# Newton's temporaries of the norms in PSUM, and two kinds of elementwise work moved from GpSimd to the vector engine

## The chip, the cores and the metric

One core of a Trainium2 chip. The metric is the device time of one execution of the program in microseconds (us); lower is better. The engines are named as the profile names them: PE is TensorE (matmuls), PEld its weight loads, DVE the vector engine, ACT the scalar engine, POOL GpSimd, SP the engine that issues most DMAs.

## What is computed

512 tokens of 1024 features go through two post-norm layers (feed forward, a mixer, feed forward, a gated addition) and then a block of attention and experts. The norms are what the change touches:

```python
def layer_norm(x, g, b):
    mu = jnp.mean(xf, axis=-1, keepdims=True)
    var = jnp.mean(jnp.square(xf - mu), axis=-1, keepdims=True)
    return (xf - mu) * lax.rsqrt(var + LN_EPS) * g + b

for i in range(DEPTH):                                   # DEPTH = 2
    h = layer_norm(DN_ALPHA * h + 0.5 * swiglu(h, ...), ln_g[i, 0], ln_b[i, 0])
    ...
    h = layer_norm(DN_ALPHA * h + mix, ln_g[i, 1], ln_b[i, 1])
    h = layer_norm(DN_ALPHA * h + 0.5 * swiglu(h, ...), ln_g[i, 2], ln_b[i, 2])
    h = h + (p[i] @ ple_w_proj[i]) * jax.nn.sigmoid(h @ ple_w_gate[i])
```

The second block begins with an RMS norm (`x * rsqrt(mean(x*x) + eps) * g`), has one before its experts, and ends with one.

## The kernel before

**Layout.** Features lie on partitions and tokens along the row, so an activation is eight tiles of 128 x 512. Every product runs in three matmuls (L258, L259, L260): both sides are split into a high part, which is a cast on ACT, and a low part, the rest after it. For weights that is `w()`: a DMA, the cast (L235, ACT) into `wh`, and the subtraction (L236) into `wl`, on DVE unless the caller names GpSimd. `wh` and `wl` are rings of six tiles each, so a cast also waits until the weight six tiles earlier is used up.

**A tail.** A norm needs sums over the features, that is, over partitions. `stat_add` keeps two running sums over the eight tiles, of the values (L308) and of their squares (square on ACT, L299; addition on DVE, L309). `tail` does the last four feature tiles in two halves of 256 tokens. When the first half of all four is done, and the first tile of the second, `sums` adds the running sums over the partitions by matmuls against ones (L316 for values, L317 for squares), which gives 128 x 2 values in a PSUM bank, and `rstd` turns these into one over the deviation and the scaled mean: a chain of 17 instructions of 128 x 2 elements on DVE, each using the result of one before it (L348 to L354 for the variance, L324 to L335 for three Newton steps by `rsqrt`, L357 for the mean). `diagonals` (L383) writes the results onto diagonals, `spread` (L374) multiplies those by ones, so that every partition has the values of all tokens, and the norm is two DVE operations (L425, L426), two on ACT (L429, L430) and a subtraction on POOL (L434) for each tile. Meanwhile PE works on the second half. Its chain is cut into steps that are put between the norm operations of the first half, and its spread comes inside the first products of the next phase (`dense_halves`), whose first half of tokens needs only the first half of the norm.

**Which tails there are.** Six layer norms: at 376 us (feed forward, then the first mixer), 597 (mixer, then feed forward), 974 (feed forward, then the gated addition), and the same three in the second layer at 1410, 1650 and 2026. A seventh tail, at 2099, is the RMS norm after the last gated addition; its chain has 13 instructions and no sum of values. The router's norm and the last norm use the same code without halves.

**Who does what.** In the halves of a tail, the addition to the sum of values (L308) runs on POOL, and so do the low parts (L236) of the third and fourth of the four weights that `opening` fetches for a phase's first products; those of the first two run on DVE. There are seven openings with four weights each.

**Order.** The code is traced as written, and a scheduler then sets the order on each engine by its own estimate of durations; each engine runs its list strictly in that order.

Of the kernel before, what the change touches and what calls it, by code (L numbers as in the profile page):

```python
# [139 lines left out]
class K:  # L140
# [17 lines left out]
    def begin(self):  # L158
        """The input, its splits, and the first weights, by what the first products need."""
# [58 lines left out]
    def old(self, j):  # L218
        """Room of long use: tables of the states, then distances and masks, then the routing."""
# [19 lines left out]
    def narrow(self, src, n):  # L239
        """A function that gives the weights of n columns by their number, out of wide loads of several."""  # L240
# [27 lines left out]
    def mark(self):  # L268
        """The instruction traced last."""
# [3 lines left out]
    def after(self, ins):  # L273
        """What is traced here is issued after ins (an order of issue, not a wait)."""
# [14 lines left out]
    def stat_add(self, st, y, c=FULL, mean=True):  # L289
        """Adds the columns c of y, and of its square, to the sums over the feature tiles."""  # L290
# [12 lines left out]
        if mean:  # L303
# [3 lines left out]
            else:  # L307
                (nc.vector if c == FULL else nc.gpsimd).tensor_tensor(st["s1"][:, c], st["s1"][:, c], y[:, c], ALU.add)  # L308
# [11 lines left out]
    def rsqrt(self, v, n):  # L320
        """1 / sqrt(v) by Newton's steps from a guess by the exponent; a generator, a step at a time."""
        nc = self.nc
        i, y, h, q = self.sm(n, I32), self.sm(n, I32), self.sm(n), self.sm(n)
        nc.vector.tensor_scalar(i, v.bitcast(I32), 1, None, op0=ALU.arith_shift_right)  # L324
        yield
        nc.vector.tensor_scalar(y, i, -1.0, 1597463007.0, op0=ALU.mult, op1=ALU.add)  # L326
        yield
        nc.vector.tensor_scalar(h, v, -0.5, None, op0=ALU.mult)  # L328
        y = y.bitcast(F32)
        for _ in range(3):  # L330
            nc.vector.tensor_tensor(q, y, y, ALU.mult)  # L331
            yield
            nc.vector.tensor_tensor(q, q, h, ALU.mult)  # L333
            yield
            nc.vector.scalar_tensor_tensor(y, q, 1.5, y, op0=ALU.add, op1=ALU.mult)  # L335
            yield
        return y

    def rstd(self, ps, n, eps, mean):
        """1 / deviation, and the mean in its units, negated; a generator."""  # L340
        nc = self.nc
        v = self.sm(n)
        if not mean:
            nc.vector.tensor_scalar(v, ps[:, 4:4 + n], 1.0 / D, eps, op0=ALU.mult, op1=ALU.add)
            yield
            return [(yield from self.rsqrt(v, n))]
        mu, m2, m = self.sm(n), self.sm(n), self.sm(n)
        nc.vector.tensor_scalar(mu, ps[:, :n], 1.0 / D, None, op0=ALU.mult)  # L348
        yield
        nc.vector.tensor_tensor(m2, mu, mu, ALU.mult)  # L350
        yield
        nc.vector.scalar_tensor_tensor(v, ps[:, 4:4 + n], 1.0 / D, m2, op0=ALU.mult, op1=ALU.subtract)
        yield
        nc.vector.tensor_scalar(v, v, 0.0, eps, op0=ALU.max, op1=ALU.add)  # L354
        yield
        r = yield from self.rsqrt(v, n)
        nc.vector.scalar_tensor_tensor(m, mu, -1.0, r, op0=ALU.mult, op1=ALU.mult)  # L357
        return [r, m]
# [8 lines left out]
    def spread(self, cs, dg=None):  # L367
        """Columns [P, 2] of per-token values, each as rows of 256 tokens on every partition, side by side."""
# [17 lines left out]
    def tail(self, st, work, norm, mean=True, end=lambda: None):  # L386
        """The last four feature tiles of a sum and the norm over all, in halves of the tokens: while work(i, half) of the second half runs,
        the first half is normalised. The norm of the second half waits in self.pending."""
# [28 lines left out]
    def layer_norm(self, y, H, g, b):  # L417
        """The norm, in place, and its splits to H, for tail()."""
# [27 lines left out]
    def dense_halves(self, ws, H, then=None):  # L446
        """dense() for up to four weights over H, whose second half of the tokens may be pending. then: called for each half."""
# [15 lines left out]
    def opening(self, srcs):  # L463
        """The weights of a phase's first products."""
        return [self.w(src, 1024, self.nc.gpsimd if n > 1 else None) for n, src in enumerate(srcs)]

# [8 lines left out]
    def ffn(self, X, H, i, ln, then=None, ws=None):  # L475
        """then: called some way before the end. ws: the first weights."""
# [78 lines left out]
    def ple(self, X, H, i, norm=None):  # L555
        """norm: column of the gains of an RMS norm that follows."""
# [96 lines left out]
    def s5_prep(self):  # L653
# [32 lines left out]
        # f = (a - 1) / lambda  # L686
# [18 lines left out]
        # powers a^2 .. a^8  # L705
# [26 lines left out]
        # phase and decay tables over the 64 chunks  # L732
# [18 lines left out]
        # stacked power tables  # L751
# [86 lines left out]
    def s5(self, uT, q):  # L838
        """z for the 128 channels of quarter q, features on partitions; a generator, a stage at a time."""
# [1240 lines left out]
```

## Time and profile before

| | |
|---|---|
| time of three runs | 2836.44, 2845.91 (median), 2849.08 us |
| span of the profiled execution | 2846.9 us |
| mean granted TensorE clock | 0.970 of full |
| PE busy | 2696.5 us, 95% |
| DVE busy | 1494.1 us, 52% |
| ACT busy | 987.0 us, 35% |
| POOL busy | 431.8 us, 15% |

The profile is of one execution; its span is within 0.1% of the median, so what follows is added up against 2846.9 us. The engines work side by side: PE is the one that is nearly always busy, and the others matter where PE waits for them. A wait shows as idle time in front of an instruction, with the instruction that ended it. Durations of DVE instructions in the timeline include time in which the instruction had started and could not go on.

### The profile page before, as it was taken

How to read it: one execution, taken by the hardware profiler on the slowest of the kernel's cores; microseconds unless marked ns; L12 is line 12 of the kernel's file. 1: busy time of each engine (PE TensorE's matmuls, PEld its weight loads, DVE VectorE, ACT ScalarE, POOL GpSimd, SP SyncE). 2: the span in 40 equal slices, each digit the busy share in tenths (PEclk: the TensorE clock that was granted, in tenths of full speed). 3: DMA queues.
4: the chain of work that ended last, by engine and by line, in shares of the span. 5: the costliest groups of instructions: out<-in, count | busy, mean ns of one | idle time of the engine just before them, and what ended most of it. 6: DMA issues, size and time to landing. Idle time of an engine off the chain costs nothing. (4 is left out here: it accounts for less than half of the span.)

```text
span 2846.9 us, 37003 instructions
## 1 busy us (share of the span) xinstructions
PE 2696.5 (95%) x14221; PEld 2170.3 (76%) x14221; DVE 1494.1 (52%) x2966; ACT 987.0 (35%) x1717; POOL 431.8 (15%) x441
## 2 busy tenths in 40 slices
PE   9999989999999899999987999999889999969996
PEld 8888888888888798888875788888788777754443
DVE  5856364564333555333589663333677666553435
ACT  4332242343222353222252452222445544322111
POOL 2101031030000140000157030000234222010000
PEclk9999998999999999999998999999999999979998
DMA  6434216523233223223231123333233222669994
GB/s 216 151 118 142 89 60 182 160 66 113 97 95 96 91 69 119 95 90 98 81 108 62 60 74 98 92 103 93 72 101 110 92 78 79 221 211 364 398 400 156
DMA packets 123826, 370.14 MB, mean 130 GB/s; under 512 B 14592, under 2 KB 14656, under 8 KB 123648
## 3 DMA queue, kind: packets, MB, share of 16 engines
q1 hardware_dynamic: 112688, 333.10, 35.2%
q0 software_dynamic: 10384, 33.61, 3.2%
q8 instruction: 112, 1.84, 0.3%
q10 hardware_dynamic: 576, 1.05, 0.1%
q14 instruction: 66, 0.54, 0.1%
HBM read 343.32 MB, written 24.39 MB: 129 GB/s over the span
## 5 line engine op out<-in xcount | busy, mean ns | idle before, releaser
L258 PE MATMUL p<-a,wh 128*128 128x512 f32 (+1 forms) x3480 | 1276.6, 367 | 0.0
L259 PE MATMUL p<-a,wh 128*128 128x512 f32 (+1 forms) x3480 | 1264.6, 363 | 0.1
L260 PE MATMUL p<-a,wl 128*128 128x512 f32 (+1 forms) x3480 | 1263.6, 363 | 0.0
L235 ACT CAST wh<-wr 128x1024 fp32r<-128x1024 f32 (+2 forms) x399 | 409.1, 1031 | 1109.9 <-PE p L259 786.0
L258 PEld LDWEIGHTS p<-a,wh 128*128 128x128 f32 x3480 | 665.3, 191 | 111.2 <-issue 8.6
L259 PEld LDWEIGHTS p<-a,wh 128*128 128x128 f32 x3480 | 666.1, 191 | 102.4 <-issue 3.6
L260 PEld LDWEIGHTS p<-a,wl 128*128 128x128 f32 x3480 | 665.2, 191 | 101.2 <-issue 1.2
L236 DVE TENSOR_TENSOR wl<-wr,wh 128x1024 fp32r<-128x1024 f32 (+1 forms) x366 | 444.7, 1218 | 405.3 <-ACT wh L235 359.7
L308 POOL TENSOR_TENSOR a<-a,a 128x256 f32<-128x256 f32 x48 | 35.1, 732 | 1328.5 <-DVE a L504 815.2
L497 DVE TENSOR_TENSOR a<-a,p 128x512 f32<-128x512 f32 x88 | 60.5, 687 | 252.4 <-PE p L260 242.7
L504 DVE SCALAR_TENSOR_TENSOR a<-p,a 128x512 f32<-128x512 f32 (+1 forms) x112 | 68.8, 614 | 200.4 <-PE p L260 200.4
L1178 ACT ACTIVATE a<-a,s 128x256 f32<-128x256 f32 (+3 forms) x128 | 67.2, 526 | 73.3 <-DVE s L1176 73.2
L829 POOL DMA_DIRECT2D spill<-a x76 | 42.5, 561 | 330.3 <-DVE a L1448 98.1
L253 DVE TENSOR_TENSOR a<-a,a 128x512 fp32r<-128x512 f32 x120 | 81.9, 689 | 9.8 <-ACT a L252 9.5
L236 POOL TENSOR_TENSOR wl<-wr,wh 128x1024 fp32r<-128x1024 f32 (+1 forms) x33 | 78.8, 2392 | 44.7 <-ACT wh L235 44.7
L299 ACT ACTIVATE a<-a 128x256 f32<-128x256 f32 (+1 forms) x93 | 45.2, 487 | 98.1 <-DVE a L504 44.2
L252 ACT CAST a<-a 128x512 fp32r<-128x512 f32 x120 | 73.6, 621 | 15.5 <-DVE a L497 6.6
L434 POOL TENSOR_TENSOR a<-a,a 128x256 fp32r<-128x256 f32 x96 | 71.5, 759 | 48.3 <-ACT a L430 47.8
L429 ACT ACTIVATE a<-a,vec 128x256 f32<-128x256 f32 x96 | 56.3, 599 | 64.3 <-DVE a L426 64.3
L1908 PE MATMUL p<-we,a 128*64 128x512 f32 x288 | 63.7, 592 | 0.0
L1947 PE MATMUL p<-a,sel 128*128 128x512 f32 x256 | 62.0, 398 | 0.1
L309 DVE TENSOR_TENSOR a<-a,a 128x256 f32<-128x256 f32 (+1 forms) x87 | 53.5, 615 | 12.5 <-ACT a L299 12.1
(423 smaller groups left out, 2523.8 us busy)
## 6 DMA issues: line engine op xcount, KB each, us to landing
wr<-in_w_dram SPq DMA_DIRECT2D x204, 512.0 KB
we<-in_wgu_dram SPq DMA_DIRECT2D x72, 512.0 KB
wr<-in_w_dram SPq DMA_DIRECT2D x64, 448.0 KB
a<-in_wgu_dram SPq DMA_DIRECT2D x112, 256.0 KB
spill<-a POOLq DMA_DIRECT2D x76, 256.0 KB, 3.4
a<-spill SPq DMA_DIRECT2D x76, 256.0 KB
we<-in_wd_dram SPq DMA_DIRECT2D x36, 512.0 KB
wr<-in_win_dram SPq DMA_DIRECT2D x31, 512.0 KB
```

What stands on the lines that cost most here:

```text
L235: nc.scalar.copy(hi[:, :n], raw[:, :n])
L236: (low or nc.vector).tensor_tensor(lo[:, :n], raw[:, :n], hi[:, :n].bitcast(F32), ALU.subtract)
L252: self.nc.scalar.copy(hi[:, :n], x)
L253: (low or self.nc.vector).tensor_tensor(lo[:, :n], x, hi[:, :n].bitcast(F32), ALU.subtract)
L258: mm(o, l[0], r[0], start=start, stop=False)
L259: mm(o, l[0], r[1], start=False, stop=False)
L260: mm(o, l[1], r[0], start=False, stop=stop)
L434: nc.gpsimd.tensor_tensor(l[:, c], y[d - 2][:, c], h[:, c].bitcast(F32), ALU.subtract)
L504: nc.vector.scalar_tensor_tensor(Y[d][:, c], o[:, c], 0.5, Y[d][:, c], op0=ALU.mult, op1=ALU.add)
L1178: nc.scalar.activation(s[x], s[x], AF.Exp, bias=nm[:, x:x + 1], accum_out=z[:, x:x + 1])
L1908: nc.tensor.matmul(o[CAP * i:CAP * i + CAP], xT[k // 4][:, a:a + CAP], wg[k], start=k == 0, stop=k == DT - 1)
L1947: nc.tensor.matmul(o, sels[b][:n, j * P:(j + 1) * P], y[h][i][:n], start=b + i == 0, stop=i == 1 and b == len(blocks) - 1)
```

## The change

`rstd` and `rsqrt` keep the variance, minus half of it and the product in each Newton step in unused columns of the PSUM bank that holds the sums; the guess, the mean and its square stay in SBUF. The formulas are rescaled so that each instruction has at most one input from PSUM and the count stays the same: 17 with a mean, 13 without. (The last norm calls `rsqrt` without a bank and keeps SBUF temporaries.) `stat_add` puts the addition to the sum of values on DVE in the halves too, and `opening` no longer names GpSimd for the low parts.

```diff
@@ stat_add
-                (nc.vector if c == FULL else nc.gpsimd).tensor_tensor(st["s1"][:, c], st["s1"][:, c], y[:, c], ALU.add)
+                nc.vector.tensor_tensor(st["s1"][:, c], st["s1"][:, c], y[:, c], ALU.add)
@@ rstd, rsqrt
-    def rsqrt(self, v, n):
-        i, y, h, q = self.sm(n, I32), self.sm(n, I32), self.sm(n), self.sm(n)
-        nc.vector.tensor_scalar(i, v.bitcast(I32), 1, None, op0=ALU.arith_shift_right)
-        nc.vector.tensor_scalar(y, i, -1.0, 1597463007.0, op0=ALU.mult, op1=ALU.add)
-        nc.vector.tensor_scalar(h, v, -0.5, None, op0=ALU.mult)
-        for _ in range(3):
-            nc.vector.tensor_tensor(q, y, y, ALU.mult)
-            nc.vector.tensor_tensor(q, q, h, ALU.mult)
-            nc.vector.scalar_tensor_tensor(y, q, 1.5, y, op0=ALU.add, op1=ALU.mult)
-    def rstd(self, ps, n, eps, mean):
-        v = self.sm(n)
-        mu, m2, m = self.sm(n), self.sm(n), self.sm(n)
-        nc.vector.tensor_scalar(mu, ps[:, :n], 1.0 / D, None, op0=ALU.mult)
-        nc.vector.tensor_tensor(m2, mu, mu, ALU.mult)
-        nc.vector.scalar_tensor_tensor(v, ps[:, 4:4 + n], 1.0 / D, m2, op0=ALU.mult, op1=ALU.subtract)
-        nc.vector.tensor_scalar(v, v, 0.0, eps, op0=ALU.max, op1=ALU.add)
-        r = yield from self.rsqrt(v, n)
-        nc.vector.scalar_tensor_tensor(m, mu, -1.0, r, op0=ALU.mult, op1=ALU.mult)
+    def rstd(self, ps, n, eps, mean):
+        v, h, q = (ps[:, 16 + 8 * x:16 + 8 * x + n] for x in range(3))
+        s1, s2 = ps[:, :n], ps[:, 4:4 + n]
+            mu, m2 = self.sm(n), self.sm(n)
+            nc.vector.tensor_scalar(mu, s1, -1.0 / D, None, op0=ALU.mult)
+            nc.vector.tensor_tensor(m2, s1, mu, ALU.mult)
+            nc.vector.tensor_tensor(v, s2, m2, ALU.add)
+            nc.vector.tensor_scalar(v, v, 0.0, D * eps, op0=ALU.max, op1=ALU.add)
+            nc.vector.tensor_scalar(v, s2, D * eps, None, op0=ALU.add)
+        r = yield from self.rsqrt(v, n, (h, q))
+        nc.vector.tensor_tensor(m, mu, r, ALU.mult)
+    def rsqrt(self, v, n, room=None):
+        h, q = room or (self.sm(n), self.sm(n))
+        y = self.sm(n)
+        nc.vector.tensor_scalar(q.bitcast(I32), v.bitcast(I32), 1, None, op0=ALU.arith_shift_right)
+        nc.vector.tensor_scalar(y.bitcast(I32), q.bitcast(I32), -1.0, 1597463007.0, op0=ALU.mult, op1=ALU.add)
+        nc.vector.tensor_scalar(h, v, -0.5, None, op0=ALU.mult)
+        for k in (1.0, 1.0, math.sqrt(D)):
+            nc.vector.tensor_tensor(q, h, y, ALU.mult)
+            nc.vector.scalar_tensor_tensor(q, q, k, y, op0=ALU.mult, op1=ALU.mult)
+            nc.vector.scalar_tensor_tensor(y, q, 1.5 * k, y, op0=ALU.add, op1=ALU.mult)
@@ opening
-        return [self.w(src, 1024, self.nc.gpsimd if n > 1 else None) for n, src in enumerate(srcs)]
+        return [self.w(src, 1024) for src in srcs]
@@ the last norm
-        ts(v, v, 1.0 / D, 1e-6, op0=ALU.mult, op1=ALU.add)
+        ts(v, v, D * 1e-6, None, op0=ALU.add)
```

Since the scheduler orders the instructions anew, they move. POOL's list loses 62 rows (48 L308 and 14 L236); DVE's gains them. The lines of the changed kernel are a few numbers off: its chain is L328 to L334 (variance), L350 to L360 (Newton), L342 (mean); L387 is the diagonals, L429 and L430 the norm, L508 the sum with the product (L504 before), L378 the spread.

The vector engine in the first tail, just after the sums of the first half, before the change (`p` are PSUM banks, `s` small tiles, `a` activations, `w` weights; numbers are buffers):

```order
L504 SCALAR_TENSOR_TENSOR a_359<-p_3171,a_359 128x256
L348 TENSOR_SCALAR s_3204<-p_3198 128x2
L350 TENSOR_TENSOR s_3205<-s_3204 128x2
L352 SCALAR_TENSOR_TENSOR s_3203<-p_3198,s_3205 128x2
L354 TENSOR_SCALAR s_3203<-s_3203 128x2
L324 TENSOR_SCALAR s_3211<-s_3203 128x2
L309 TENSOR_TENSOR a_2921<-a_2921,a_3194 128x256
L326 TENSOR_SCALAR s_3212<-s_3211 128x2
L328 TENSOR_SCALAR s_3213<-s_3203 128x2
L331 TENSOR_TENSOR s_3214<-s_3212 128x2
L333 TENSOR_TENSOR s_3214<-s_3214,s_3213 128x2
```

and in the changed kernel, from the same place:

```order
L508 SCALAR_TENSOR_TENSOR a_359<-p_3171,a_359 128x256
L328 TENSOR_SCALAR s_3203<-p_3198 128x2
L308 TENSOR_TENSOR a_2954<-a_2954,a_359 128x256
L330 TENSOR_TENSOR s_3204<-p_3198,s_3203 128x2
L236 TENSOR_TENSOR wl_3392<-wr_3390,wh_3391 128x1024
L309 TENSOR_TENSOR a_2921<-a_2921,a_3194 128x256
L332 TENSOR_TENSOR p_3198<-p_3198,s_3204 128x2
L508 SCALAR_TENSOR_TENSOR a_361<-p_3224,a_361 128x256
L334 TENSOR_SCALAR p_3198<-p_3198 128x2
L308 TENSOR_TENSOR a_2954<-a_2954,a_361 128x256
L350 TENSOR_SCALAR p_3198<-p_3198 128x2
L236 TENSOR_TENSOR wl_3398<-wr_3396,wh_3397 128x1024
```

Behind each of the two L236 there (third and fourth weight of the opening) stand steps of the chain, and the additions of the sum of values (L308) stand between them; the chain's operands are now `p`.

The vector engine at the end of the second half's chain in the same tail, before and after; the two `wl` are the weights that follow the opening's:

```order
L333 TENSOR_TENSOR s_3352<-s_3352,s_3351 128x2
L335 SCALAR_TENSOR_TENSOR s_3350<-s_3352,s_3350 128x2
L357 SCALAR_TENSOR_TENSOR s_3334<-s_3332,s_3350 128x2
L236 TENSOR_TENSOR wl_3559<-wr_3557,wh_3558 128x1024
L383 TENSOR_SCALAR a_3450<-const,s_3350 128x128 x2
L383 TENSOR_SCALAR a_3450<-const,s_3334 128x128 x2
```

```order
L356 TENSOR_TENSOR p_3312<-p_3312,s_3343 128x2
L358 SCALAR_TENSOR_TENSOR p_3312<-p_3312,s_3343 128x2
L236 TENSOR_TENSOR wl_3551<-wr_3549,wh_3550 128x1024
L360 SCALAR_TENSOR_TENSOR s_3343<-p_3312,s_3343 128x2
L236 TENSOR_TENSOR wl_3557<-wr_3555,wh_3556 128x1024
L342 TENSOR_TENSOR s_3375<-s_3327,s_3343 128x2
L387 TENSOR_SCALAR a_3442<-const,s_3343 128x128 x2
```

One L236 stood between the chain and the diagonals, the other behind them; now both stand ahead of the diagonals.

PE among the first products of the next phase, where the second half's spread stands (the `ones` row), before and after; `a_3033` to `a_3036` are the sixth and seventh feature tile's split:

```order
L260 MATMUL p_3410<-a_3033,wl_3388 128x256
L258 MATMUL p_3411<-a_3033,wh_3393 128x256
L259 MATMUL p_3411<-a_3034,wh_3393 128x256
L374 MATMUL p_3455<-a_3450,ones 128x512
L260 MATMUL p_3411<-a_3033,wl_3394 128x256
L258 MATMUL p_3412<-a_3033,wh_3399 128x256
L259 MATMUL p_3412<-a_3034,wh_3399 128x256
```

```order
L260 MATMUL p_3402<-a_3035,wl_3380 128x256
L258 MATMUL p_3403<-a_3035,wh_3385 128x256
L259 MATMUL p_3403<-a_3036,wh_3385 128x256
L260 MATMUL p_3403<-a_3035,wl_3386 128x256
L378 MATMUL p_3447<-a_3442,ones 128x512
L258 MATMUL p_3404<-a_3035,wh_3391 128x256
L259 MATMUL p_3404<-a_3036,wh_3391 128x256
```

The spread stands 13 matmuls later in the products than before; there were 30 matmuls between it and the first that needs the second half of the norm, and there are 18.

## Rows read from the trace of the kernel before

**Rows 1.** The page's part 1: engine, busy us (share of the span) x instructions.
```profile
PE 2696.5 (95%) x14221; PEld 2170.3 (76%) x14221; DVE 1494.1 (52%) x2966; ACT 987.0 (35%) x1717; POOL 431.8 (15%) x441
```
**Rows 2.** PE's waits over the whole span: us in total, times, longest.
```profile
PE p L374 <- DVE a L383: 36.1, 10, 5.2
...
PE p L316 <- POOL a L308: 8.3, 6, 1.4
...
PE p L317 <- DVE a L309: 6.6, 3, 4.2
```
**Rows 3.** Timeline of DVE, first tail: start, duration (us), instruction, [idle before <-releaser].
```profile
376.71 0.16 DVE L348 TENSOR_SCALAR s<-p 128x2 f32<-128x2 f32 x1 [0.36 <-PE p L317]
...
377.21 0.16 DVE L352 SCALAR_TENSOR_TENSOR s<-p,s 128x2 f32<-128x2 f32 x1
377.40 2.14 DVE L354 TENSOR_SCALAR s<-s 128x2 f32<-128x2 f32 x1
...
382.59 2.26 DVE L357 SCALAR_TENSOR_TENSOR s<-s,s 128x2 f32<-128x2 f32 x1
384.77 0.47 DVE L383 TENSOR_SCALAR a<-const,s 128x128 f32<-128x128 f32 x2
...
396.21 0.65 DVE L354 TENSOR_SCALAR s<-s 128x2 f32<-128x2 f32 x1
```
**Rows 4.** Timeline of POOL, same tail.
```profile
377.12 2.41 POOL L236 TENSOR_TENSOR wl<-wr,wh 128x1024 fp32r<-128x1024 f32 x1
...
382.49 2.34 POOL L236 TENSOR_TENSOR wl<-wr,wh 128x1024 fp32r<-128x1024 f32 x1
...
391.82 0.73 POOL L308 TENSOR_TENSOR a<-a,a 128x256 f32<-128x256 f32 x1 [4.65 <-DVE a L504]
```
**Rows 5.** Timelines of ACT and PE, same tail: a cast, and PE's first and second spread.
```profile
379.25 1.05 ACT L235 CAST wh<-wr 128x1024 fp32r<-128x1024 f32 x1 [2.04 <-issue]
...
381.40 0.28 PE L259 MATMUL p<-a,wh 128*128 128x256 f32 x1
381.52 0.28 PE L260 MATMUL p<-a,wl 128*128 128x256 f32 x1
386.03 1.67 PE L374 MATMUL p<-a,ones 128*128 128x512 f32 x2 [4.22 <-DVE a L383]
...
403.68 1.13 PE L374 MATMUL p<-a,ones 128*128 128x512 f32 x2 [1.84 <-DVE a L383]
```
**Rows 6.** DVE groups by line and shape: busy, mean ns | idle before.
```profile
L348 DVE TENSOR_SCALAR s<-p 128x2 f32<-128x2 f32 x12 | 1.9, 160 | 10.5 <-PE p L317 10.5
```
**Rows 7.** Timelines of DVE and PE, tail at 974 us (feed forward, then gated addition).
```profile
974.75 0.16 DVE L352 SCALAR_TENSOR_TENSOR s<-p,s 128x2 f32<-128x2 f32 x1
974.83 1.22 DVE L236 TENSOR_TENSOR wl<-wr,wh 128x1024 fp32r<-128x1024 f32 x1
975.97 0.42 DVE L309 TENSOR_TENSOR a<-a,a 128x256 f32<-128x256 f32 x1
976.31 0.16 DVE L354 TENSOR_SCALAR s<-s 128x2 f32<-128x2 f32 x1
...
992.26 2.63 DVE L309 TENSOR_TENSOR a<-a,a 128x256 f32<-128x256 f32 x1
...
994.95 0.58 PE L317 MATMUL p<-ones,a 128*128 128x1 f32 x2 [1.20 <-DVE a L309]
```
**Rows 8.** Stretches: us, engines' busy us, PEclk (granted clock), DMA share, GB/s.
```profile
386.30:389.60 3.30, 3.30 (x12) 2.46 (x12) 1.83 (x7) 1.02 (x2) 0.72 (x1) 0.53 0.70 238
...
993.90:1000.50 6.60, 5.55 (x16) 4.68 (x17) 5.40 (x18) 3.22 (x9) 4.79 (x7) 0.51 0.23 79
...
614.90:621.50 6.60, 6.57 (x32) 6.44 (x31) 4.77 (x17) 4.14 (x10) 4.35 (x7) 0.52 0.00 0
392.60:396.50 3.90, 3.87 (x30) 3.66 (x31) 2.60 (x9) 2.52 (x7) 3.29 (x5) 1.00 0.01 4
```
**Rows 9.** Timeline of DVE, tail at 2099 us (the RMS norm).
```profile
2108.95 1.22 DVE L236 TENSOR_TENSOR wl<-wr,wh 128x1024 fp32r<-128x1024 f32 x1
```

More of the change, by code (lines that the diff above doesn't have):

```diff
@@ L318, in sums @@
         return ps
-    def rsqrt(self, v, n):
+    def rstd(self, ps, n, eps, mean):
         nc = self.nc
-        i, y, h, q = self.sm(n, I32), self.sm(n, I32), self.sm(n), self.sm(n)
-        nc.vector.tensor_scalar(i, v.bitcast(I32), 1, None, op0=ALU.arith_shift_right)
-        yield
-        nc.vector.tensor_scalar(y, i, -1.0, 1597463007.0, op0=ALU.mult, op1=ALU.add)
+        v, h, q = (ps[:, 16 + 8 * x:16 + 8 * x + n] for x in range(3))
+        s1, s2 = ps[:, :n], ps[:, 4:4 + n]
+        if mean:
+            mu, m2 = self.sm(n), self.sm(n)
+            nc.vector.tensor_scalar(mu, s1, -1.0 / D, None, op0=ALU.mult)
+            yield
+            nc.vector.tensor_tensor(m2, s1, mu, ALU.mult)
+            yield
+            nc.vector.tensor_tensor(v, s2, m2, ALU.add)
+            yield
+            nc.vector.tensor_scalar(v, v, 0.0, D * eps, op0=ALU.max, op1=ALU.add)
+        else:
+            nc.vector.tensor_scalar(v, s2, D * eps, None, op0=ALU.add)
+        yield
+        r = yield from self.rsqrt(v, n, (h, q))
+        if not mean:
+            return [r]
+        m = self.sm(n)
+        nc.vector.tensor_tensor(m, mu, r, ALU.mult)
+        return [r, m]
@@ L327, in rsqrt @@
+    def rsqrt(self, v, n, room=None):
+        nc = self.nc
+        h, q = room or (self.sm(n), self.sm(n))
+        y = self.sm(n)
+        nc.vector.tensor_scalar(q.bitcast(I32), v.bitcast(I32), 1, None, op0=ALU.arith_shift_right)
+        yield
+        nc.vector.tensor_scalar(y.bitcast(I32), q.bitcast(I32), -1.0, 1597463007.0, op0=ALU.mult, op1=ALU.add)
         yield
         nc.vector.tensor_scalar(h, v, -0.5, None, op0=ALU.mult)
-        y = y.bitcast(F32)
-        for _ in range(3):
-            nc.vector.tensor_tensor(q, y, y, ALU.mult)
+        for k in (1.0, 1.0, math.sqrt(D)):
+            nc.vector.tensor_tensor(q, h, y, ALU.mult)
@@ L332, in rsqrt @@
             yield
-            nc.vector.tensor_tensor(q, q, h, ALU.mult)
+            nc.vector.scalar_tensor_tensor(q, q, k, y, op0=ALU.mult, op1=ALU.mult)
             yield
-            nc.vector.scalar_tensor_tensor(y, q, 1.5, y, op0=ALU.add, op1=ALU.mult)
+            nc.vector.scalar_tensor_tensor(y, q, 1.5 * k, y, op0=ALU.add, op1=ALU.mult)
             yield
         return y
-    def rstd(self, ps, n, eps, mean):
-        nc = self.nc
-        v = self.sm(n)
[L343 to L346, printed above, removed]
-        mu, m2, m = self.sm(n), self.sm(n), self.sm(n)
-        nc.vector.tensor_scalar(mu, ps[:, :n], 1.0 / D, None, op0=ALU.mult)
-        yield
-        nc.vector.tensor_tensor(m2, mu, mu, ALU.mult)
-        yield
-        nc.vector.scalar_tensor_tensor(v, ps[:, 4:4 + n], 1.0 / D, m2, op0=ALU.mult, op1=ALU.subtract)
-        yield
-        nc.vector.tensor_scalar(v, v, 0.0, eps, op0=ALU.max, op1=ALU.add)
-        yield
-        r = yield from self.rsqrt(v, n)
-        nc.vector.scalar_tensor_tensor(m, mu, -1.0, r, op0=ALU.mult, op1=ALU.mult)
-        return [r, m]
```

## The prediction

> **What bounds the kernel now.** The page's first part comes first: PE is busy for 95% of the span, DVE for half of it [rows 1]. Work on DVE or POOL therefore counts only where PE waits for it. The list of PE's waits gives the size of what this change can reach: 36.1 us at ten spreads, 8.3 at six sums of values, 6.6 at three sums of squares [rows 2], 51 us of 2846.9. Three of the ten spreads are second halves with a wait like the 1.84 of the first tail, seven are first halves with waits like 4.22 there [rows 5]. The rest of the time is products, and stays.
>
> Next comes what DVE did ahead of the first spread of the first tail. The steps of 128 x 2 take 0.16 us, but two of them, L354 and L357, took 2.14 and 2.26 [rows 3]. Each of these lies in a low part on POOL, from 377.12 for 2.41 and from 382.49 for 2.34 [rows 4], and ends with it. L352 started inside the same POOL operation and took 0.16 [rows 3]: it reads PSUM, and L354 and L357 have all their inputs in SBUF. L348, which always reads PSUM, has a mean of 160 ns over twelve [rows 6]. So a DVE step with inputs in SBUF alone stands still while POOL does an addition or a subtraction, and one with an input in PSUM does not. The change takes both ends of this: the steps go to PSUM, and POOL's low parts go to DVE. No DVE instruction of the kernel before writes PSUM.
>
> **The first spreads.** Prices in the order of the list: a step that needs the one before it starts 0.19 us after it (377.21 to 377.40) [rows 3]. Between instructions that don't need each other a step occupies DVE for 0.08, a low part for 1.14, an addition of 256 columns for 0.34 (the starts 974.75, 974.83, 975.97, 976.31) [rows 7]. In the changed list the first chain is mixed with three L308, three L309 and both low parts that POOL had, so few steps wait for the one before. The first tail, from 376.71 on: three steps, L308, a low part and L309 fill 0.24 + 0.34 + 1.14 + 0.34 = 2.06, to 378.8. Then two L508/L308 pairs' worth of work can run, but the second low part needs its cast, which started at 379.25 for 1.05 [rows 5], so 380.30; it waited for PE to be done with an older tile, and that stays. Low part to 381.44. Three more steps and three additions, 1.26: 382.70. Nine steps that each need the one before, at 0.195: 384.46. From the first diagonal to the spread it was 1.26 (384.77 [rows 3] to 386.03 [rows 5]) with an addition in it, so 0.92 without: 385.4. It was 386.03. **0.6 saved**, of the two stalls of some 2.0 each: the rest goes back to two low parts and three additions that now stand ahead of the diagonals. The same reckoning gives 0.4 in the two tails after a mixer, and 0.5 in the two at 974 and 2026, where three low parts stand ahead of the spread. Six tails: 3.0.
>
> **The sums in the middle.** PE waits at L316 for the addition on POOL, 0.73 long [rows 4]. On DVE it is 0.34 to 0.42 [rows 7], but comes behind up to one norm operation of the same length. Taken as 0.2 less, six times: 1.2; the bounds are 0 and 0.4 each. At 992.26 an L309 of 0.42 took 2.63 under a low part on POOL, and L317 then waited 1.20 [rows 7]; with POOL's low parts gone this wait goes in both such tails: 2.4.
>
> **The second spreads.** At 1.84 [rows 5] three of them wait for a chain that had a stalled step, 0.65 at 396.21 [rows 3], and a low part in it; 5.5 in all, and it goes. But the spread stands later among the products, 18 matmuls ahead of the first that needs the second half, not 30. Matmuls of 256 columns start 0.12 apart (381.40, 381.52 [rows 5]), so the cover is 18 x 0.12 = 2.2 for a norm that needs several operations of 0.34, some 2.8 with the way through ACT (an estimate from eight such operations). Two low parts ahead of the diagonals lengthen the chain by 1.14 against the 1.4 that thirteen later matmuls give. I charge 0.3 in three tails: 4.6 gained; the bounds are 5.5 and, with a wait of 0.8 in all six tails, 0.7.
>
> **The RMS tail.** Its values' low parts stay on POOL, so the stall moves to another instruction there, and one low part more, 1.22 long at 2108.95 [rows 9], stands ahead of the diagonals, while the spread comes six matmuls later (0.7). I charge 0.7 lost; bounds 0 and 1.2.
>
> **The clock.** Behind some of the waits PE ran at half clock: 6.6 us at 0.51 from 993.9 and 6.6 at 0.52 from 614.9, while from 392.6, where there had been one wait of 1.4 alone, it was at 1.00 [rows 8]. At full clock 30 matmuls took 3.87, so the 32 at 614.9 would take 4.1: such a stretch costs 2.4. The two after a pair of waits, at 974's tail and its sister, lose the second wait. Whether that is enough is not shown: I credit one of the two, 2.4. The stretch from 386.3 at 0.53 [rows 8] follows the first spread's wait, which hardly shrinks, and stays.
>
> Sum: 3.0 + 1.2 + 2.4 + 4.6 - 0.7 + 2.4 = 12.9. The profiled span is 2846.9 and the median 2845.9, so the same to 1 us; from the median, 2833.
>
> **Writing PSUM.** A step that writes PSUM and is read by the next is in no row. From above it is bounded by a stalled small step, 0.65 [rows 3]; from below by the 0.16 of L348 [rows 6], so a little below the price taken. I take the 0.19 of dependent steps, since L352, which reads PSUM and depends on the step before, kept to it. [...]
>
> **Rivals.** *A, DVE takes over what POOL's lock had cost.* The chain queues behind a low part that waits for a late cast, and behind six additions. If that costs 0.6 more than reckoned, the first spreads gain nothing (0); if the spread's later place adds a wait of 0.8 in all six, the second ones gain 0.7; the sums 3.6, the RMS tail -0.7, the clock nothing: 3.6 gained, **2842**. For it: DVE's list is strict, and the cast at 379.25 follows PE. Against: the places are taken up with independent work that has to be done anyway.
>
> *B, the clock.* With fewer and shorter waits no stretch behind a second half falls to half clock: the second of the two, and the two tails at 597 and 1650, 2.4 each, are 7.2 more, and products at full clock bring tiles and casts sooner, some 0.3 at each first spread: 9 more, **2824**. For it: one wait of 1.4 alone kept 1.00 [rows 8]. Against: 614.9 fell behind a wait of the same sort [rows 8], which only shrinks by 0.2.
>
> *C, slower: PSUM is dear to write and read back.* At 0.65 a step, not 0.20, nine dependent steps in six first chains add 0.45 x 54 = 24, and in the three second chains that have no slack 0.45 x 27 = 12: 36 - 13 = 23 lost, **2869**. It decides from 0.16 more a step (13 / 81), and passes the bound of a change that can be told from 0.34. For it: no row shows such a write. Against: reading shows no such price.
>
> *D, the change doesn't do what it says.* The mean (L342), the diagonals (L387) and L309 still read SBUF alone. If POOL's subtractions of the norm (L434) stop them as its low parts did, by the 0.5 that the 0.65 of row 396.21 had over 0.16 [rows 3], two such in six chains lose 6.0 and L317's 2.4 stays: 2.1 gained, **2844**. Against: in the first chains L434 has not begun when the diagonals are written.
>
> **How the numbers follow.** 0.5%, 14 us, is about what a measurement of this kernel can tell from no change: below 2832 counts as faster, above 2860 as slower. Chances: the forecast 0.41, A 0.23, B 0.22, C 0.09, D 0.05. The forecast lies at the border; with its unknowns (clock 0 to 4.8, second spreads 0.7 to 5.5) a little under half of it, 0.19, falls beyond. Faster: 0.22 + 0.19 = 0.41. Slower: 0.09. Within: 0.50. The range leaves out C and the outer parts of A and B: 2820, half of B's distance below it, to 2848, somewhat beyond A and D.
>
> **What would show it.** Steps on `p` of the chain at 0.16 with starts 0.19 apart confirm the price of PSUM; starts 0.3 or more apart are C. The first spread of the first tail should stand at 385.4 with a wait of 3.6; 4.2 or more, with a low part or its cast last, is A. The second spreads should have lost their 1.84, with at most 0.3 at the first matmul of the second half. L317 should not wait at 994. The granted clock from 993.9 and 614.9 tells forecast from B. An L387, L342 or L309 of over 0.6 under a POOL row is D. I am wrong most easily in the second spread's place and in the clock, since small waits decide both.

## The result, and the profile after

The changed kernel takes 2827.2 us (median of four runs, 2826.2 to 2832.9) against 2847.5 for the kernel before: a ratio of 0.9937, 95% interval 0.9921 to 0.9953. Run a second time beside other kernels it took 2827.0, ratio 0.9943 (0.9923 to 0.9962). The forecast was 2833, range 2820 to 2848. The profiled execution has a span of 2831.0 us; before it was 2846.9.

First the engines, the page's part 1 of the changed kernel (columns as in [rows 1]):

```profile
PE 2692.0 (95%) x14221; PEld 2169.9 (77%) x14221; DVE 1481.7 (52%) x3028; ACT 985.0 (35%) x1717; POOL 367.0 (13%) x379
```

PE's idle time is the span less its busy time: 2846.9 - 2696.5 = 150.4 before [rows 1], 2831.0 - 2692.0 = 139.0 now. So 11.4 us of the 15.9 that the profiled span lost are waits. The other 4.5 are the same matmuls done in less busy time; the mean granted clock rose from 0.970 to 0.973 of full. This split is used for all kernels below, since spans alone mix the two. The medians lie 20.3 apart, 4.4 more than the profiled spans: the profiled execution was the longest of the four timed, and the last section shows a stretch that can make such a difference.

The waits of PE in the tails, from the list of waits (total, times, longest), to be held against [rows 2]:

```profile
PE p L378 <- DVE a L387: 28.0, 7, 5.8
PE p L316 <- DVE a L308: 7.1, 6, 1.2
...
PE p L317 <- DVE a L309: 4.2, 1, 4.2
PE p L259 <- POOL a L438: 0.9, 4, 0.3
```

Ten waits at the spreads have become seven: the second halves no longer wait there. The two waits of 1.2 at the sums of squares are gone (6.6 to 4.2). The last line is new: products of the next phase wait for the low part of a norm, four times, 0.9 in all.

The vector engine ahead of the first spread of the first tail, and that spread on PE (timeline; columns as in [rows 3]):

```profile
377.08 0.16 DVE L328 TENSOR_SCALAR s<-p 128x2 f32<-128x2 f32 x1 [0.36 <-PE p L317]
...
377.56 1.22 DVE L236 TENSOR_TENSOR wl<-wr,wh 128x1024 fp32r<-128x1024 f32 x1
...
380.71 1.22 DVE L236 TENSOR_TENSOR wl<-wr,wh 128x1024 fp32r<-128x1024 f32 x1
...
382.25 0.16 DVE L354 TENSOR_SCALAR p<-p 128x2 f32<-128x2 f32 x1
...
383.31 0.16 DVE L360 SCALAR_TENSOR_TENSOR s<-p,s 128x2 f32<-128x2 f32 x1
383.50 0.17 DVE L356 TENSOR_TENSOR p<-p,s 128x2 f32<-128x2 f32 x1
...
384.70 0.16 DVE L342 TENSOR_TENSOR s<-s,s 128x2 f32<-128x2 f32 x1
384.78 0.87 DVE L387 TENSOR_SCALAR a<-const,s 128x128 f32<-128x128 f32 x4
```

```profile
385.70 1.13 PE L378 MATMUL p<-a,ones 128*128 128x512 f32 x2 [3.53 <-DVE a L387]
```

No step is long any more; those that write `p` take 0.16 to 0.17 and follow each other at 0.19 to 0.20. What stands in place of the two stalls (steps that had started and could not go on) are the two low parts of 1.22, and the wait is 3.53 instead of 4.22 [rows 5].

### The profile page after: what moved, and what is told of

Read it like the earlier page. It is cut to its first block, busy times and chain, and to the rows that moved or that the text cites. A ratio compares the mean times of both kernels' runs of the same rounds, so it can differ in the third digit from the quotient of the medians.

```text
span 2831.0 us, 36993 instructions
## 1 busy us (share of the span) xinstructions
PE 2692.0 (95%) x14221; PEld 2169.9 (77%) x14221; DVE 1481.7 (52%) x3028; ACT 985.0 (35%) x1717; POOL 367.0 (13%) x379
## 3 DMA queue, kind: packets, MB, share of 16 engines
q1 hardware_dynamic: 112688, 333.10, 36.1%
q8 instruction: 112, 1.84, 0.3%
## 5 line engine op out<-in xcount | busy, mean ns | idle before, releaser
L259 PE MATMUL p<-a,wh 128*128 128x512 f32 (+1 forms) x3480 | 1263.7, 363 | 0.9 <-POOL a L438 0.9
L259 PEld LDWEIGHTS p<-a,wh 128*128 128x128 f32 x3480 | 665.6, 191 | 103.3 <-issue 3.8
L236 DVE TENSOR_TENSOR wl<-wr,wh 128x1024 fp32r<-128x1024 f32 (+2 forms) x380 | 461.1, 1217 | 410.4 <-ACT wh L235 365.9
L508 DVE SCALAR_TENSOR_TENSOR a<-p,a 128x512 f32<-128x512 f32 (+1 forms) x112 | 68.8, 614 | 204.9 <-PE p L260 204.9
L429 DVE TENSOR_TENSOR a<-a,p 128x256 f32<-128x256 f32 x96 | 39.8, 415 | 36.5 <-PE p L378 36.5
L1935 ACT ACTIVATE a<-p,wgt 128x512 fp32r<-128x512 f32 x32 | 22.0, 687 | 104.7 <-PE p L1933 102.1
L1951 PEld LDWEIGHTS p<-a,sel 128*128 128x128 f32 x256 | 47.4, 188 | 11.8 <-issue 0.8
```

Source lines behind the costliest of these rows:

```text
L236: (low or nc.vector).tensor_tensor(lo[:, :n], raw[:, :n], hi[:, :n].bitcast(F32), ALU.subtract)
L259: mm(o, l[0], r[1], start=False, stop=False)
L508: nc.vector.scalar_tensor_tensor(Y[d][:, c], o[:, c], 0.5, Y[d][:, c], op0=ALU.mult, op1=ALU.add)
L1951: nc.tensor.matmul(o, sels[b][:n, j * P:(j + 1) * P], y[h][i][:n], start=b + i == 0, stop=i == 1 and b == len(blocks) - 1)
```

## The experiments

Line numbers of the experiments differ by a few where lines were added: the spread is L374 to L383, the diagonals L383 to L392. "Waits" is span less PE busy time of the profiled execution.

**Parts of the change alone.** Four kernels were run side by side: each takes the kernel before and adds one part, or both moves.

The PSUM temporaries alone, that is, the changed kernel with these two lines put back:

```diff
-                nc.vector.tensor_tensor(st["s1"][:, c], st["s1"][:, c], y[:, c], ALU.add)
+                (nc.vector if c == FULL else nc.gpsimd).tensor_tensor(st["s1"][:, c], st["s1"][:, c], y[:, c], ALU.add)
...
-        return [self.w(src, 1024) for src in srcs]
+        return [self.w(src, 1024, self.nc.gpsimd if n > 1 else None) for n, src in enumerate(srcs)]
```

> The kernel before with the chain's temporaries in PSUM alone; the running sums and the opening's low parts stay on GpSimd. Theory (what stalls is any DVE instruction whose inputs lie in SBUF, beside an addition or subtraction on POOL; the steps on PSUM no longer stall, but an L309, the mean and the diagonals still can): the steps of the chain take 0.16 us also under a low part on POOL, one L309 or the mean takes over 1.5 us there instead, the first spreads gain 0.8 us each (5), the second spreads lose part of their 1.84 (2 to 4), the waits at the sums of 1.39 and 1.20 stay: 6 to 9 us faster than before. Rival (the PSUM temporaries carry the whole gain, the moves nothing): the first spreads gain as in the changed kernel and more, 18 to 20 us faster than before, level with the changed kernel.

Measured: 2840.3 us, ratio 0.9974 (0.9961 to 0.9987); waits 141.7, 8.7 less than before. By time that is 4.8 us, less than the 6 to 9 expected, and PE's busy time did not fall (2698.5 against 2696.5). DVE in the first tail, and POOL beside it (timelines):

```profile
377.26 2.42 DVE L309 TENSOR_TENSOR a<-a,a 128x256 f32<-128x256 f32 x1
379.60 0.15 DVE L350 TENSOR_SCALAR p<-p 128x2 int32<-128x2 int32 x1
...
382.16 0.17 DVE L358 SCALAR_TENSOR_TENSOR p<-p,s 128x2 f32<-128x2 f32 x1
382.36 0.16 DVE L360 SCALAR_TENSOR_TENSOR s<-p,s 128x2 f32<-128x2 f32 x1
382.55 1.70 DVE L342 TENSOR_TENSOR s<-s,s 128x2 f32<-128x2 f32 x1
```

```profile
377.00 2.39 POOL L236 TENSOR_TENSOR wl<-wr,wh 128x1024 fp32r<-128x1024 f32 x1
...
381.72 2.52 POOL L236 TENSOR_TENSOR wl<-wr,wh 128x1024 fp32r<-128x1024 f32 x1
```

This is the mechanism in one place. Under the second low part, L358 and L360, with one input in PSUM and the other in SBUF, take 0.17 and 0.16, and the next instruction, L342, with both in SBUF, stands until that low part ends (384.25 against 384.24). L309 stands under the first and ends 0.3 after it. The stall is not cured here, it goes to the next instruction that reads SBUF alone: 2.42 at L309 and 1.70 at L342, where L354 and L357 had taken 2.14 and 2.26 [rows 3]. The first spread waits 3.41 all the same, as in the changed kernel.

Both moves alone, temporaries in SBUF:

```diff
-                (nc.vector if c == FULL else nc.gpsimd).tensor_tensor(st["s1"][:, c], st["s1"][:, c], y[:, c], ALU.add)
+                nc.vector.tensor_tensor(st["s1"][:, c], st["s1"][:, c], y[:, c], ALU.add)
...
-        return [self.w(src, 1024, self.nc.gpsimd if n > 1 else None) for n, src in enumerate(srcs)]
+        return [self.w(src, 1024) for src in srcs]
```

> The kernel before with both moves to the vector engine (low parts of the openings, running sums) and the chain's temporaries left in SBUF. Theory (with nothing left on POOL in the first halves there is nothing that stalls a chain in SBUF): steps of 0.16 us in the first chains, first spreads as in the changed kernel within 0.3 us, L316 waits 1.18, L317 at the tail after 974 us no longer waits; in the second chains steps still stall beside the norm's subtractions on POOL by some 0.4 to 0.6 each, which costs up to 1 us at three second spreads, and the RMS tail is longer by one stalled step: 14 to 18 us faster than before. Rival (the PSUM temporaries carry the gain): under 5 us faster than before, with the first spreads waiting as long as before.

Measured: 2831.0 us, ratio 0.9939 (0.9917 to 0.996); waits 135.8, 14.6 less than before and 3.2 less than the changed kernel has. The chain in SBUF, first tail, and PE's waits:

```profile
380.75 0.16 DVE L354 TENSOR_SCALAR s<-s 128x2 f32<-128x2 f32 x1
...
384.09 0.16 DVE L331 TENSOR_TENSOR s<-s 128x2 f32<-128x2 f32 x1
384.28 0.16 DVE L333 TENSOR_TENSOR s<-s,s 128x2 f32<-128x2 f32 x1
```

```profile
PE p L374 <- DVE a L383: 26.4, 8, 4.8
PE p L316 <- DVE a L308: 7.1, 6, 1.2
```

With POOL quiet in the first half, L354, which took 2.14 [rows 3], takes 0.16 in SBUF too. The steps are as fast as in PSUM and the first spreads wait a little less (3.38 in the first tail). One second spread still waits, 1.07. The moves carry the gain; the rival's "under 5 us" is out.

The low parts alone (the second pair of those lines), and the sums alone (the first pair):

> The kernel before with the openings' low parts on the vector engine alone. Theory: the two stalls of 2 us in each first chain are gone, in their place stand two low parts of 1.14 and stalls of up to 0.7 beside the running sums on POOL, so the first spreads gain 0 to 0.5 us each; L316 keeps its 1.39; L317 loses its 1.20 twice; second spreads keep most of their 1.84: 4 to 8 us faster than before. Rival (the low parts on POOL are all that mattered): 14 us or more faster.

> The kernel before with the running sums of the values on the vector engine alone. Theory: the stalls beside the low parts on POOL stay, and the low parts on POOL no longer queue behind a running sum and start earlier; L316 waits 1.18 instead of 1.39 (1.2 us in six tails); first spreads within 0.5 us of before: 0 to 4 us faster. Rival: the sums on POOL were the main cost, 8 us or more faster.

Measured: low parts 2831.9 us, ratio 0.9947 (0.9928 to 0.9966), waits 140.8; sums 2840.9 us, ratio 0.998 (0.9967 to 0.9992), waits 145.8. The waits at the spreads, with the low parts moved and then with the sums moved:

```profile
PE p L374 <- DVE a L383: 28.0, 10, 4.8
PE p L316 <- POOL a L308: 8.3, 6, 1.4
```

```profile
PE p L374 <- DVE a L383: 33.0, 8, 5.5
...
PE p L316 <- DVE a L308: 7.1, 6, 1.2
```

With the low parts on DVE the first spread of the first tail waits 3.11, less than in the other three and in the changed kernel. Three additions fewer stand in DVE's list there, which may be why (not shown by a run of its own); the stalls beside the sums that stay on POOL are short (0.27 to 0.67 us for a stalled instruction with its own time). A stalled step there, and one in the kernel with the sums moved:

```profile
382.31 0.59 DVE L333 TENSOR_TENSOR s<-s,s 128x2 f32<-128x2 f32 x1
```

```profile
378.48 2.36 DVE L350 TENSOR_TENSOR s<-s 128x2 f32<-128x2 f32 x1
```

I had expected 4 to 8 us from the low parts. The time fell by 13, of which 9.6 are waits: the expectation took too little off the first spreads (0 to 0.5 each, measured 1.1). The rival, 14 or more from the low parts, lies inside the interval (10 to 20 us) and is not excluded. For the sums, 4 us were at the edge of what was expected.

**The place of the temporaries, timed directly.** The changed kernel and the one with both moves alone were run again on one chip.

> The changed kernel once more, on one chip with the next two, to compare them directly. Theory and rival alike: 2826 to 2833 us; it is the measure for the other two.

> Once more the kernel before with both moves and temporaries in SBUF. Theory (the moves carry the gain, and with them done the place of the temporaries is worth nothing that can be measured): within 4 us of the changed kernel run beside it. Rival (the temporaries in PSUM carry a part of their own, as the second spreads' wait of 1.07 us would suggest): the changed kernel is faster by more than 4 us.

Measured: 2827.0 (2823.3 to 2834.5) and 2830.6 (2829.1 to 2830.7); ratios to before 0.9943 (0.9923 to 0.9962) and 0.995 (0.9932 to 0.9969). The difference is 3.6 us, inside the bound of 4 and inside both intervals. By waits the one in SBUF is ahead (135.3 against 139.4), by time the one in PSUM. What the PSUM temporaries add to the moves can't be told from nothing here.

**The low parts behind the diagonals.** Next the list in which the low parts of an opening may not come ahead of the first half's diagonals (`self.after` sets an order of issue):

```diff
             if i == 2:
                 dg = self.diagonals(rm)
+                self.dgm = self.mark()
...
-        (low or nc.vector).tensor_tensor(lo[:, :n], raw[:, :n], hi[:, :n].bitcast(F32), ALU.subtract)
+        with self.after(self.dgm) if held and self.dgm else nullcontext():
+            (low or nc.vector).tensor_tensor(lo[:, :n], raw[:, :n], hi[:, :n].bitcast(F32), ALU.subtract)
...
-        return [self.w(src, 1024) for src in srcs]
+        return [self.w(src, 1024, held=True) for src in srcs]
```

> The changed kernel, with the low parts of each opening ordered behind the diagonals of the first half (an order of issue on the vector engine, nothing else). Theory (what is left of the first spreads' wait, 3.0 to 4.6 us, is the low parts that stand ahead of the diagonals, 1.14 each): the chain then ends with the addition that waits for PE's last product ahead of the spread, the first spreads wait 1.3 to 1.6 us in all six tails, 2 us less in four and 3 less in two: 14 us less waiting than the changed kernel, 2810 to 2816 us. Rival (DVE only pushes the work on: the low parts are then late for the next phase's products, or the sums in the middle and the second spreads wait instead): 2823 to 2831, with new waits at L316, at the first products or at the second spreads.

Measured: 2805.7 us (2802.5 to 2815.9), ratio 0.9876 (0.985 to 0.9902): better than both kernels and than the 2810 to 2816 expected. Its waits are 126.6, 12.4 less than the changed kernel's, where 14 were expected. PE's waits, and the first tail around the second addition of a product and the diagonals:

```profile
PE p L380 <- DVE a L389: 12.5, 7, 5.8
PE p L318 <- DVE a L310: 7.1, 6, 1.2
...
PE p L261 <- POOL a L441: 5.0, 11, 1.0
```

```profile
379.52 0.43 DVE L511 SCALAR_TENSOR_TENSOR a<-p,a 128x256 f32<-128x256 f32 x1 [0.65 <-PE p L262]
...
382.06 0.42 DVE L511 SCALAR_TENSOR_TENSOR a<-p,a 128x256 f32<-128x256 f32 x1
382.39 0.15 DVE L344 TENSOR_TENSOR s<-s,s 128x2 f32<-128x2 f32 x1
382.46 0.87 DVE L389 TENSOR_SCALAR a<-const,s 128x128 f32<-128x128 f32 x4
...
383.91 1.22 DVE L238 TENSOR_TENSOR wl<-wr,wh 128x1024 fp32r<-128x1024 f32 x1
```

The spreads went from 28.0 to 12.5, 15.5 less; 4.1 came back at the first products of the next phase, which wait longer for the norm's low parts on POOL (0.9 to 5.0). The rival had expected waits there, but for the weights' low parts and as large as the gain. The rest of the first spread's wait, 1.38 in the first tail, has the chain behind an L511 that waits 0.65 for PE at 379.52.

The same kernel with the additions of the third and fourth tiles held as well (`part` under the same `self.after`), and then that one with the low parts of the values' weights moved from GpSimd to DVE in the RMS tail:

```diff
-        ws = [self.w(A["winv"][:, k * 408:(k + 2) * 408], 816, nc.gpsimd) for k in range(0, 8, 2)]
+        ws = [self.w(A["winv"][:, k * 408:(k + 2) * 408], 816, held=True) for k in range(0, 8, 2)]
```

> As the kernel with the low parts held, and the additions of the products of the third and fourth second-half tiles are ordered behind the diagonals as well. Theory: the first spreads of the four or six tails concerned wait under 0.5 us, 1 us less each than with the low parts held alone: 2804 to 2811. Rival (PE then waits for the later additions in the middle, at L316): no better than with the low parts held alone.

> As the last one, and the low parts of the values' weights in the RMS tail run on the vector engine, behind that tail's diagonals, instead of on GpSimd. Theory (two L309 of 0.42 took 2.56 and 2.06 there under these low parts): the RMS tail's first spread waits 2 to 3 us instead of 5.75, all else the same: 2 to 4 us less waiting than the last kernel. Rival (that spread waits for the products and sigmoids ahead of it, not for stalled additions): within 1 us of the last kernel.

Measured: 2814.7 us, ratio 0.9896 (0.9874 to 0.9918), waits 126.4; and 2809.4 us, ratio 0.9872 (0.9849 to 0.9894), waits 121.1. Holding the additions took nothing off the waits (126.6 to 126.4) and gained no time: the first spread waits 1.18 instead of 1.38, where I had expected under 0.5. The addition that the chain stands behind is the second one, at 379.52 above, and that one was not held. Moving the values' low parts took 5.3 us of waits: the RMS tail's first spread waits 1.1, not 5.75, and for another engine, which is more than expected. In the changed kernel an L309 stood there for 2.06 beside such a low part, DVE and POOL:

```profile
2086.05 2.06 DVE L309 TENSOR_TENSOR a<-a,a 128x256 f32<-128x256 f32 x1
```

```profile
2085.71 2.12 POOL L236 TENSOR_TENSOR wl<-wr,wh 128x816 fp32r<-128x816 f32 x1
```

And the low parts held with the temporaries in SBUF, the kernel before with both moves and the same order:

> The kernel before with both moves and the low parts held behind the diagonals, temporaries in SBUF. Theory (with POOL quiet in the first halves it makes no difference where the temporaries lie): first spreads within 0.3 us of those of the kernel with temporaries in PSUM and the low parts held; what is left between the two are stalls in the second halves, 0 to 2 us each at three second spreads: 0 to 6 us slower than that one. Rival: the PSUM temporaries are what shortens the chain, first spreads wait over 1 us longer each, over 8 us slower.

Measured: 2815.8 us (2803.4 to 2816.6), ratio 0.9886 (0.9861 to 0.9911), waits 123.6. Its first spread waits 0.38 in the first tail, 1.0 less than with PSUM (0.3 was the expected difference), so the rival is out: PSUM does not shorten the chain. By median it is 10 us behind the kernel with PSUM, and by waits 3 ahead. That need not be a cost of SBUF: the runs of both kernels lie in the same two groups, 2802 to 2806 and 2815 to 2817, three of five in the lower one with PSUM and one of five with SBUF, so the medians fall in different groups. The profiled executions come from different groups too: what separates them is not the waits but PE's own busy time, 2690.1 at a mean granted clock of 0.976 against 2674.1 at 0.981, which leads to the clock.

**The clock by itself.** In this one PE does useless work in the first spread's wait, and the products behind that spread are kept behind it:

```diff
-            self.mm3(o, (w[0][:, s], w[1][:, s]), x, start and k == 0, stop and k == len(xs) - 1)
+            with self.after(self.held) if self.held else nullcontext():
+                self.mm3(o, (w[0][:, s], w[1][:, s]), x, start and k == 0, stop and k == len(xs) - 1)
...
         with self.after(self.last_mm):
+            for _ in range(fill):
+                nc.tensor.matmul(o[:, :P], self.ones, self.ones, start=True, stop=True)
             nc.tensor.matmul(o[:, :n], self.ones, dg[:, :n], start=True, stop=True)
...
-                rm = self.spread(rm, dg)
+                rm = self.spread(rm, dg, 12)
+                self.held = self.mark()
```

> The changed kernel with 12 useless matmuls of 128 columns (ones by ones, into the bank that the spread then overwrites) on PE ahead of the spread of the first half in all seven tails, so that PE works through some 2.5 us of a wait that it has anyway; all other work is in the same order on PE and DVE. Theory (the half clock behind the tails comes from PE's waits, and is worth more than the wait that the change removed): the first spreads start at the same place in the work, their wait is 2.5 us shorter and filled, and most of the half-clock stretches behind the first spreads, some 40 us of them in the changed kernel's six norm tails, are gone: 8 to 16 us faster than the changed kernel. Rival (the clock falls for another reason, the matmuls only take room): no faster than the changed kernel, with the same stretches at half clock.

Measured: 2815.8 us (2810.0 to 2818.5), ratio 0.9894 (0.9874 to 0.9914), 11.2 below the changed kernel run beside it. PE in the first tail, and stretches of that kernel with the granted clock behind the busy times (PEclk, third from the end):

```profile
382.13 2.84 PE L381 MATMUL p<-ones 128*128 128x128 f32 x24
385.82 1.12 PE L382 MATMUL p<-a,ones 128*128 128x512 f32 x2 [0.84 <-DVE a L391]
```

```profile
383.00:398.00 15.00, 12.98 (x103) 12.11 (x102) 12.30 (x49) 9.21 (x20) 5.21 (x8) 1.00 0.15 54
972.00:988.00 16.00, 14.70 (x76) 12.25 (x77) 11.45 (x43) 11.82 (x25) 6.53 (x8) 1.00 0.16 52
```

The same places in the changed kernel:

```profile
386.80:390.20 3.40, 3.40 (x19) 3.40 (x18) 2.68 (x7) 1.80 (x3) 0.00 (x0) 0.53 0.00 0
393.70:397.10 3.40, 3.40 (x19) 3.40 (x18) 3.30 (x17) 3.04 (x7) 2.83 (x5) 0.52 0.00 0
...
973.90:980.70 6.80, 5.22 (x18) 4.19 (x19) 4.43 (x16) 1.20 (x2) 0.00 (x0) 0.52 0.29 78
```

Nothing reaches the spread earlier: 0.84 of wait and 2.84 of useless work make 3.7, against a wait of 3.53. Over the whole kernel it is the same: 119.7 of waits and 19.9 of useless matmuls make 139.6, against 139.0 and 139.4 in the two profiled executions of the changed kernel. The order of the other work is not quite the same (behind the first spreads a norm operation and two low parts stand elsewhere in DVE's list, and in the first tail the second spread in PE's), but the waits outside the first spreads are: 110.6 against 111.0. Yet 11 us are gone by the medians, and the granted clock is at full where it was at half. In this kernel the waits cost twice, once as waits and once in the matmuls behind the first spreads, at 0.52 to 0.53 of the clock in the stretches above and at 1.00 with the waits filled; the second part, 11.2 us by the medians, was had back without removing the waits.

**Both together:** low parts and values' low parts held, additions not, and five useless matmuls instead of twelve.

> The changed kernel with the low parts of the openings behind the diagonals, the low parts of the values' weights in the RMS tail on DVE behind its diagonals too, and five useless matmuls of 128 columns (1.1 us) on PE ahead of each first spread. Theory (less waiting and a clock that stays up add): waits as in the kernel with the values held, some 99 us, less 6 that are filled; half clock behind the tails nearly gone, the stretches from 440 to 520 us in some runs and not in others: 2798 to 2808 us. Rival (what clock there was to win is won by holding the low parts): 2805 to 2812, level with that kernel.

Measured: 2810.7 us (2806.6 to 2811.3), ratio 0.9881 (0.9863 to 0.9899), waits 116.8: 9.8 less than with the low parts held alone, but no faster. The rival's 2805 to 2812 holds. Most of the 9.8 are not gone but filled: the useless matmuls themselves take 8.9 in all. (The expectation's 99 us for the waits with the values held does not agree with that kernel's profile, 121.1.) What else is in the way stands in the last section.

## Why the prediction came out

**Waits.** The sum's terms, in the prediction's order. First spreads: 3.0 forecast; 36.1 less the three second halves of 1.84 and the RMS tail's 4.7 is 25.9 before [rows 2], 28.0 - 5.75 = 22.3 now, 3.7 gained. The middle sums: 1.2 and 2.4 forecast, 8.3 - 7.1 = 1.2 and 6.6 - 4.2 = 2.4 measured. The second spreads: 4.6 forecast, 5.5 less the new 0.9 at L259 = 4.6 (0.3 was charged in each of three tails; it came as 0.9 over four). Thirteen later matmuls at 0.12 give 1.6, not the prediction's 1.4; no term hung on it. The RMS tail: 0.7 lost by the forecast, 5.75 - 4.65 = 1.1 measured, and the stall did move to another L309 (2.06 above). Together 10.8 against 10.5. The reckoned spread of the first tail, 385.4, came at 385.70, from a chain that began 0.37 us later; that 0.37 stands between the two traces from 17 us on and has nothing to do with the tail.

**The price of PSUM.** Taken at 0.19 to 0.20 a step, measured at 0.19 to 0.20 (starts at 383.31, 383.50, 383.70 and 383.90). Rival C is out. Steps from and to PSUM took 0.16 to 0.17 us in this trace, the step of the chain in SBUF, L342, 0.16; in the kernel with both moves alone the steps in SBUF took 0.16 and started 0.19 apart (384.09 and 384.28).

**The clock** is the term that was mis-sized: 2.4 in the sum, 4.5 between the profiled executions, and 10.1 in a second profiled execution of the changed kernel (PE busy 2686.4), 5.6 of it between the two executions of that one kernel, for which a stretch far from any tail is the likely place (last section). The credit was for the second of two half-clock stretches in the tails at 974 and 2026. In the first of them that stretch did shrink, to half its length, and did not go; the changed kernel:

```profile
984.20:987.50 3.30, 3.30 (x9) 2.59 (x10) 3.16 (x16) 3.14 (x9) 2.78 (x5) 0.52 0.00 0
987.50:991.00 3.50, 3.50 (x16) 2.87 (x15) 3.22 (x13) 2.75 (x6) 3.08 (x3) 0.96 0.38 88
```

I had left the tails at 597 and 1650 out, since their waits shrank only from 3.55 and 1.38 to 3.02 and 1.18. The first of them gained most. That stretch before, in the changed kernel, and in the changed kernel's second execution:

```profile
604.70:621.70 17.00, 13.93 (x62) 12.49 (x63) 11.33 (x35) 8.16 (x18) 7.35 (x10) 0.61 0.09 31
```

```profile
601.50:618.00 16.50, 13.52 (x106) 12.84 (x107) 13.81 (x50) 9.57 (x19) 6.51 (x8) 1.00 0.13 39
```

```profile
594.60:611.10 16.50, 13.52 (x93) 12.31 (x93) 12.21 (x47) 9.57 (x19) 6.29 (x8) 0.90 0.07 28
```

62 matmuls against 106 and 93 in nearly the same busy time. The first tail, whose waits shrank as much, went the other way: half clock in two places (0.53 and 0.52 above), where before there was one, 0.53 from 386.3, and 1.00 from 392.6 [rows 8]. So no rule of which wait makes the clock fall can be read from these rows, and that the sum of it came out on the right side was in part luck. The tail at 597 is a part of rival B, which I gave 0.22.

**Rival A** (the chain behind a low part that waits for its cast) is what remains of the waits, rather than wrong: the second low part starts at 380.71, right behind its cast on ACT, and holding the low parts back took 15.5 us off the spreads.

```profile
379.62 1.05 ACT L235 CAST wh<-wr 128x1024 fp32r<-128x1024 f32 x1 [2.04 <-issue]
```

It did not decide, since the stalls that the two low parts of 1.22 replaced were longer, 2.14 and 2.26 [rows 3]. **Rival D** did not happen in the first chains (L342 0.16, L387 0.87 for four). In the second chains of the tails at 974 and 2026 an L342 took 0.50 and 0.52, and no second spread waited for it. (The 2.1 of this rival also leaves out the clock's 2.4, which its sentence does not say.)

**The reason** was right as to what stalls and what ends the stall, and left open which end of the conflict counts. In waits either one does most of it alone (8.7 less with PSUM, 14.6 with the moves), and both together have 11.4. In time PSUM alone gains 4.8 us and the moves alone 14, against 20. The kernel's gain is that of the moves, above all of the low parts.

**The chances.** Half of them, 0.50, lay within 0.5% of no change; the measured 0.63%, with an interval from 0.47% to 0.79%, falls just beyond it. The waits alone, 11.4 us or 0.40%, would have stayed within; it is the clock that carries it over (0.970 to 0.973 on the mean, 4.5 us of busy time between the profiled executions).

## What to carry to other kernels

A DVE step that takes two microseconds instead of 0.16 is looked up beside POOL's timeline first; if a POOL tensor operation covers it, taking the work off POOL helped more here than moving the step's operands to PSUM (14 us against 4.8), and doing both brought nothing that could be told over the moves alone (3.6 us, inside both intervals). Then the work that was taken over is best kept out of the chain that PE waits for: by medians an order of issue for the low parts was worth 21 us with the temporaries in PSUM and 15 with those in SBUF, some 12 of them waits in both; the whole change was worth 20. When two kernels differ by less than 0.5%, compare PE's waits and PE's busy time apart, since PE's busy time outweighed the waits here: with the low parts held, 16.0 us of busy time between the temporaries in SBUF and in PSUM (mean granted clocks 0.976 and 0.981) against 3.0 of waits the other way.

## What the runs showed of the hardware

Two executions of the same changed kernel were profiled. Their waits agree within 0.4 us (139.0 and 139.4), their spans differ by 5.2 (2831.0 and 2825.8). The stretch from 430 to 530 us, far from any tail, in the first and in the second:

```profile
430.00:530.00 100.00, 100.00 (x640) 82.76 (x639) 39.97 (x56) 26.99 (x38) 12.83 (x13) 0.90 0.57 174
```

```profile
430.00:530.00 100.00, 100.00 (x683) 83.36 (x683) 46.71 (x61) 31.77 (x44) 13.39 (x13) 1.00 0.62 190
```

At 1.00 PE did 683 matmuls there, at 0.90 640, with PE busy throughout in both; the kernel before had 0.88 and 628. Among the other kernels the profiled execution with the low parts held had 1.00 and 679, the one with the low parts and values' low parts held and filled 0.90 and 640. The second took 8.0 us longer in its profiled span: 9.8 less of waits, 8.9 more of useless matmuls, and 8.9 more of PE's other busy time, for which this stretch is the likely place. The first execution of the changed kernel (2831.0) and that with twelve useless matmuls (2814.0) both had 0.90 here; like with like, the useless matmuls are worth 17 us, more than the 11 of the medians. The runs of one kernel lie in groups 12 to 13 us apart (2802.5 and 2815.9 with the low parts held; 2803.4 and 2815.8 with SBUF temporaries held), and with the low parts held the mean granted clocks of the groups are 0.980 to 0.981 and 0.976 to 0.978. This fits the stretch; that it is this one in each of them was not shown, since only one execution of each run has a trace.
